# Packed score rows and DMA-carried splits in the second attention of a two-layer encoder

## The chip, the cores and the metric

One core of a Trainium2 chip runs the kernel. The metric is the device time of one execution in microseconds. TensorE multiplies matrices: it holds up to 128x128 weights and streams up to 512 columns past them, into banks of PSUM. VectorE (DVE), ScalarE (ACT) and GpSimd (POOL) work element by element; SyncE (SP) issues transfers. In the profile, PE is TensorE's matmuls and PEld its weight loads.

## The reference

Two layers on x of 1024 positions by 1024 features. Each computes `u = x*(1+scale)+shift` and `x = LayerNorm(alpha*x + gate*mixer(u))`. Layer 0 mixes by a dilated windowed attention of 18 heads. Layer 1, where the change lies, mixes by a latent attention of 16 heads:

```
cq, ckv, k_rope, gate = split(u @ w_in, [256, 384, 416])
q  = rmsnorm(cq) @ w_uq        # per head: 64 plain values, 32 rotary ones
kv = rmsnorm(ckv) @ w_ukv      # per head: 64 key values, 64 value columns
q_rope, k_rope = rope(q_rope), rope(k_rope)     # k_rope is shared by all heads
s  = (q_nope . k_nope + q_rope . k_rope) * 96**-0.5
y  = softmax(s) @ v * silu(gate) @ w_out
```

So a score is a dot product over 96 values: 64 of the head and 32 rotary ones.

## The kernel before, in words

Nearly every product is made from split numbers: a float32 value is held as a rounded high part h (type fp32r) and the rest l, and `mm3` (lines 90 to 94) makes a product as three matmuls, h·h, h·l and l·h. A split is a copy by ACT, which rounds, and a subtraction by DVE or POOL.

The program runs layer A's projections and attention, layer A's gate and output, then layer B. `layer_b_in` (from line 1015) makes the latents of eight blocks of 128 positions (`latents`, and `latents_t`, which transposes them), and then eight gate blocks of two halves each (`gate`, line 1116), 24 matmuls a half; `weave` (line 49) alternates two generators in proportion to their weights. The 16 heads go in eight pairs p:

- `b_turn(p)` (line 1238), once for two pairs (four heads), multiplies out the rotary part of the queries for both halves of the positions, turns it with the cosine and sine table cs, and leaves the rows in tiles `ab` and `rope`.
- `b_qk(p)` (line 1265) makes queries and keys of the pair for each half of 512 positions. A product of 128 rows holds both heads, 64 rows each; each head's rows are split by a 64-row copy and a 64-row subtraction of their own (lines 1278, 1279, 1304, 1306). The rotary rows are split by ACT (1285) and POOL (1287) into rows 64 to 127. `b_rope_rows` (1224) copies the rotary key rows of a head's tiles to the tiles of the next but one by a POOL transfer.
- `b_v` makes the values of four heads.

A head has a high and a low query tile and a high and a low key tile, each of 128 rows: 64 plain ones and 64 for the 32 rotary values and zeros. `latents_t` writes the first key rows.

`layer_b_attention` (1316) goes over 128 units u; a unit is a head and 128 of its queries. `front(u)` makes the scores of the unit against 1024 keys: `mm3` for each half of the keys, so six matmuls over 128 rows (line 1328). `soft` takes the row maximum (DVE, 1336), `expo` the exponential (ACT, 1344), `middle(u-2)` transposes the weights two units later, eight transposes, splits them into pth (ACT, 1379) and ptl (DVE, 1380), and `back` multiplies two units' weights with the values, 16 matmuls (1396), whose output ACT copies (1405, 1406). In each turn of the loop comes first `front(u)`, then `middle(u-2)`, then `expo(u)`, and in every second turn `back`. Steps of `b_turn` and `b_qk` of the next pair (the generator prep) and of `b_v` (vprep) are put between them: `b_turn` starts at unit 2 of every second pair, `b_qk` at unit 8 of a pair's 16.

PSUM holds two score tiles s of two banks each and four banks t, which transposes, outputs and up-projections share. SBUF tiles of 4 KB a row come from two pools, G with 33 and H with 14.

The order on TensorE and SP is that of the code (`FIXED`, line 42). The order on ACT, DVE and POOL is chosen when the program is built, by the readiness of the operations there with the order of the code as priority; on the chip each engine goes through its list in order. The denominators of the softmax go through DRAM: SP writes `den_d` and reads it spread over 64 rows (`spread`, lines 1358 and 1359), and POOL multiplies (1365).

Of the kernel before, what the change touches and what calls it, by code (L numbers as in the profile page):

```python
# [69 lines left out]
class Trunk:  # L70
# [944 lines left out]
    def layer_b_in(self):  # L1015
# [11 lines left out]
        self.kb = [[self.ht(F32R, "kb") for _ in range(2)] for _ in range(2)]  # L1027

# [22 lines left out]
        nc.gpsimd.memset(latn, 0.0)  # L1051
        ln = [latn[:, 0:512], latn[:, 512:1024]]

        def latents(i):
# [8 lines left out]
            tmp = self.M.tile([P, 64], F32, tag="krt", bufs=2, name=self.nm("krt"))  # L1063
# [19 lines left out]
        def latents_t(i):  # L1083
            t, c = ln[i % 2], i * P
            pt = self.bank("plt")
            for j in range(4):
                nc.tensor.transpose(pt[:, j * P : j * P + P], t[:, j * P : j * P + P], self.ident)
            dst = [(h[:, c : c + P], l[:, c : c + P], slice(0, P), j) for j, (h, l) in enumerate(self.lat)]
            for e, (h, l) in enumerate(self.kb):
                dst.append((h[64:128, c : c + P], l[64:128, c : c + P], slice(64 - 64 * e, 128 - 64 * e), 3))  # L1090
            for h, l, rows, j in dst:
                src = pt[rows, j * P : j * P + P]
                nc.scalar.copy(h, src)
                nc.vector.tensor_tensor(l, src, f32(h), op=ALU.subtract)

# [18 lines left out]
        self.wu, self.wv, self.q, self.gT = {}, {}, {}, []  # L1114
# [16 lines left out]
        for b in range(8):  # L1131
            if b + 2 < 8:
                gq[b + 2] = self.bw_load(b + 2)
            for _ in gate(b, 0, self.bank if b < 2 else self.mbank):
                pass
# [10 lines left out]
            if b == 0:  # L1146
                self.kb.append([self.ht(F32R, "kb") for _ in range(2)])
                self.b_rope_rows(2)
            if b == 1:
                gate1 = self.ada_last()  # L1150
            if b == 2:
# [3 lines left out]
                self.cs = self.ht(F32, "cs")  # L1155
                nc.sync.dma_start(self.cs, A["qtab"])
# [67 lines left out]
    def b_rope_rows(self, hd):  # L1224

        for src, dst in zip(self.kb[(hd - 2) % 3], self.kb[hd % 3]):
            self.nc.gpsimd.dma_start(dst[64:128, :], src[64:128, :])
# [9 lines left out]

    def b_turn(self, p):


        nc = self.nc
        r1 = self.ht(F32, "rope")
        self.rope = {p: [], p + 1: [r1[64:128, 0:512], r1[64:128, 512:1024]]}
        for hf in range(2):
# [10 lines left out]
            r0 = ab[64:128, 512:1024]  # L1255
            for dst, row, op in (
                (r1[64:96, sl], 32, ALU.subtract),
                (r1[96:128, sl], 96, ALU.add),
                (r0[32:64], 64, ALU.add),
                (r0[0:32], 0, ALU.subtract),  # L1260
            ):
                nc.gpsimd.tensor_tensor(dst, ab[row : row + 32, 0:512], ab[row : row + 32, 512:1024], op=op)
            self.rope[p].append(r0)

    def b_qk(self, p):

# [4 lines left out]
        qe = [self.gt(F32R, "q") for _ in range(2)]  # L1271
        qo = [self.gt(F32R, "q") for _ in range(2)]
        self.q[2 * p], self.q[2 * p + 1] = qe, qo
        ke, ko = self.kb[(2 * p) % 3], self.kb[(2 * p + 1) % 3]
        rr = self.rope.pop(p)

        def put(dst, sl, src):
            nc.scalar.copy(dst[0][0:64, sl], src)
            nc.vector.tensor_tensor(dst[1][0:64, sl], src, f32(dst[0][0:64, sl]), op=ALU.subtract)

        def rope(hf, part):
            sl = slice(hf * 512, hf * 512 + 512)
            for q in (qe, qo):
                if part == 0:
                    nc.scalar.activation(q[0][64:128, sl], rr[hf], AF.Copy)
                else:
                    nc.gpsimd.tensor_tensor(q[1][64:128, sl], rr[hf], f32(q[0][64:128, sl]), op=ALU.subtract)

        if p:
            self.b_rope_rows(2 * p)  # L1290
            self.b_rope_rows(2 * p + 1)
        for hf in range(2):
# [3 lines left out]
            put(qe, sl, ps[0:64, :])  # L1296
            put(qo, sl, ps[64:128, :])
            yield 0.0
            rope(hf, 0)
# [3 lines left out]
            for n, k in enumerate((ke, ko)):  # L1303
                nc.scalar.copy(k[0][0:64, sl], ps[64 * n : 64 * n + 64, :])
            for n, k in enumerate((ke, ko)):
                nc.vector.tensor_tensor(
                    k[1][0:64, sl], ps[64 * n : 64 * n + 64, :], f32(k[0][0:64, sl]), op=ALU.subtract
                )
            rope(hf, 1)
# [6 lines left out]
    def layer_b_attention(self):  # L1316
# [4 lines left out]
        def front(u):  # L1321
            hd, t = u // 8, u % 8
            q, k = self.q[hd], self.kb[hd % 3]
            s = self.PB.tile([P, 1024], F32, tag="s", bufs=2, name=self.nm("s"))
            ts = slice(t * P, t * P + P)
            for j in range(2):
                ks = slice(j * 512, j * 512 + 512)
                self.mm3(s[:, ks], q[0][:, ts], q[1][:, ts], k[0][:, ks], k[1][:, ks], True, True)
            if t == 7:
                self.q.pop(hd)  # L1330
            st[u] = s
# [81 lines left out]
        for u in range(nu + 4):  # L1413
            p, r = u // 16, u % 16
            if u < nu:
                front(u)
                next(prep, None)
                next(vprep, None)
                soft(u)
            if p + 1 < NPAIR_B:  # L1420
                if r == 1:
                    self.b_weights(p + 1)
                if p % 2 and r == 2:
                    prep = self.b_turn(p + 1)
                if r == 8:
                    prep = self.b_qk(p + 1)
            elif u < nu:
                if r in (1, 3, 5, 7):
                    self.b_wo_load((r - 1) // 2)
                elif r in (4, 6, 8, 10):  # L1430
                    self.b_wo_split((r - 4) // 2, nc.gpsimd)
                if r in (10, 11, 12, 13):
                    self.b_yt(r - 10, 0)
                elif r in (14, 15):
                    for b in (2 * r - 24, 2 * r - 23):
                        self.b_wo_load(b)
            if 0 <= u - 2 < nu:
                middle(u - 2)
                next(vprep, None)
            if u < nu:  # L1440
                expo(u)
            if u == nu:
                self.b_rows()
                self.b_out_blocks(0, range(4))
            if u == nu + 1:
                self.b_out_blocks(1, range(4))
            if u >= 4 and u % 2 == 0 and u < nu + 4:
                back((u - 4) // 2)
            if u >= 11 and u % 4 == 3:
                normalise((u - 11) // 4)  # L1450
            if u % 32 == 2 and 32 < u < nu:
# [228 lines left out]
```

## Time and profile before

| | before |
|---|---|
| median of 3 runs | 1356.2 us (1355.8 to 1360.3) |
| the profiled execution | 1356.85 us, span 1355.1 |
| TensorE clock granted | 0.994 of full speed |
| second attention, first to last score | 776.0 to 1244.0 us |
| scores (tile s, lines 92 to 94) | 768 matmuls |
| their row maximum | 128 times, 1217 ns |
| their exponential | 128 times, 1126 ns |
| DMA queues, all stages | 114.30 MB, mean 84 GB/s |

A row of the groups names line, engine, operation, output and inputs, shapes and count, then busy time and the mean duration of one in ns, then the idle time of the engine just before them and what ended it. A row of busy time by stage has the stretch, its length, and for each engine busy time and instructions. A row of the instructions in order of time has start and duration in us. A row of the waits has who waited for whom, the sum, how often, and the longest.

### The profile page before, as it was taken

What the parts mean: (1) busy time and instruction counts of PE and PEld (TensorE: products, weight loads), DVE (VectorE), ACT (ScalarE), POOL (GpSimd) and SP (SyncE); (2) the same over time, 40 slices, a digit from 0 to 9 for tenths busy, and PEclk for the clock granted to TensorE, in tenths of its full rate; (3) what the DMA queues carried; (4) which work ended last, traced back from release to release, by engine and by line L of the source; (5) the groups of instructions that cost most, each with busy time, mean ns of one, the idle gap of its engine ahead of it and who ended that gap; (6) DMA issues with size and microseconds to landing.
All of it is one profiled execution on the core that took longest, in us unless ns stands there. A gap on an engine that the chain in (4) does not pass through costs nothing.

```text
span 1355.1 us, 20458 instructions
## 1 busy us (share of the span) xinstructions
PE 1328.6 (98%) x7435; PEld 1143.5 (84%) x7435; DVE 855.9 (63%) x1480; ACT 799.1 (59%) x1631; POOL 565.3 (42%) x552
## 2 busy tenths in 40 slices
PE   9999999999999999999999999999999999999997
PEld 7888888888888888888988888898889889898776
DVE  7645445445544345376733378878787788777887
ACT  4665556544444423165632397889698878887411
POOL 0333123213231477425533444734654473444861
PEclk8999999999999999999999999999999999999999
DMA  9423211113244374371163011111121111113322
GB/s 369 146 35 64 33 58 54 49 27 126 96 132 132 92 179 160 124 252 47 50 182 115 2 33 34 24 38 25 32 52 28 30 25 28 25 55 124 110 93 93
DMA packets 45117, 114.30 MB, mean 84 GB/s; under 512 B 6893, under 2 KB 13342, under 8 KB 45017
## 3 DMA queue, kind: packets, MB, share of 16 engines
q1 hardware_dynamic: 40204, 100.41, 24.0%
q0 software_dynamic: 4192, 12.27, 3.7%
q8 instruction: 59, 0.97, 0.3%
q14 instruction: 42, 0.34, 0.1%
q10 hardware_dynamic: 620, 0.31, 0.1%
HBM read 96.43 MB, written 8.67 MB: 78 GB/s over the span
## 4 chain that ended last, share of the span: by engine, by line
PE 78%; DVE 7%; ACT 7%; DMA 3%; issue 3%; SPq 0%; ACTq 0%; DVEq 0%
PE pj L92 8%; PE pj L94 8%; PE pj L93 8%; PE o L1396 6%; PE t L1376 5%; PE po L92 4%; PE po L93 4%; PE po L94 4%; PE s L92 3%; PE s L94 3%; PE s L93 3%; PE pg L92 2%; PE pg L93 2%; PE pg L94 2%; PE ip L272 2%
## 5 line engine op out<-in xcount | busy, mean ns | idle before, releaser
L92 PE MATMUL pj<-uh,wh 128*128 128x512 f32 x528 | 217.2, 411 | 0.7 <-ACT wh L104 0.7
L94 PE MATMUL pj<-uh,wl 128*128 128x512 f32 x528 | 207.0, 392 | 0.0
L93 PE MATMUL pj<-ul,wh 128*128 128x512 f32 x528 | 206.8, 392 | 0.0
L1336 DVE TENSOR_REDUCE mb<-s 128x1 f32<-128x1024 f32 x128 | 155.8, 1217 | 48.7 <-PE s L94 47.9
L1380 DVE TENSOR_TENSOR ptl<-t,pth 128x512 fp32r<-128x512 f32 x256 | 165.3, 681 | 5.2 <-ACT pth L1379 3.0
L1379 ACT CAST pth<-t 128x512 fp32r<-128x512 f32 x256 | 139.5, 590 | 37.4 <-PE t L1376 34.0
L1344 ACT ACTIVATE pr<-s,mb 128x1024 f32<-128x1024 f32 x128 | 144.2, 1126 | 15.4 <-DVE mb L1336 14.7
L105 POOL TENSOR_TENSOR wl<-wraw,wh 128x1024 fp32r<-128x1024 f32 x42 | 106.3, 2536 | 102.4 <-ACT wh L104 75.4
L1376 PEld LDWEIGHTS t<-ident,pr 128*128 128x128 f32 x1024 | 119.3, 141 | 19.1 <-DVE ptl L1380 2.8
L1376 PE MATMUL t<-ident,pr 128*128 128x128 f32 x1024 | 133.1, 273 | 2.1 <-DVE ptl L1380 2.1
L1396 PE MATMUL o<-pth,vq 128*128 128x256 f32 x512 | 130.4, 292 | 1.1 <-DVE ptl L1380 1.1
L1396 PE MATMUL o<-ptl,vq 128*128 128x256 f32 x512 | 125.6, 283 | 0.8 <-DVE ptl L1380 0.5
L564 ACT ACTIVATE sb<-sb,stat 128x256 f32<-128x256 f32 (+1 forms) x144 | 67.0, 466 | 94.8 <-DVE stat L558 94.7
L94 PEld LDWEIGHTS pj<-uh,wl 128*128 128x128 f32 x528 | 99.1, 188 | 22.2
L1407 POOL TENSOR_TENSOR osum<-osum 64x256 f32<-64x256 f32 x64 | 47.9, 748 | 163.7 <-ACT osum L1406 162.6
L92 PEld LDWEIGHTS pj<-uh,wh 128*128 128x128 f32 x528 | 99.7, 189 | 15.1 <-ACT wh L104 1.1
L93 PEld LDWEIGHTS pj<-ul,wh 128*128 128x128 f32 x528 | 99.8, 189 | 14.0
L92 PE MATMUL s<-kb,q 128*128 128x512 f32 x256 | 105.8, 413 | 0.1
L94 PE MATMUL s<-kb,q 128*128 128x512 f32 x256 | 100.4, 392 | 0.0
L93 PE MATMUL s<-kb,q 128*128 128x512 f32 x256 | 100.4, 392 | 0.0
L1396 PEld LDWEIGHTS o<-ptl,vq 128*128 128x128 f32 x512 | 97.8, 191 | 1.7 <-DVE ptl L1380 1.7
L1396 PEld LDWEIGHTS o<-pth,vq 128*128 128x128 f32 x512 | 97.6, 191 | 1.8 <-DVE ptl L1380 1.7
(289 smaller groups left out, 3128.2 us busy)
## 6 DMA issues: line engine op xcount, KB each, us to landing
wraw<-wa SPq DMA_DIRECT2D x36, 512.0 KB
ada<-ada_row SPq DMA_DIRECT2D x64, 256.0 KB
wraw<-wo_a SPq DMA_DIRECT2D x18, 512.0 KB
ada<-ada_ss SPq DMA_DIRECT2D x16, 512.0 KB
kb<-kb POOLq DMA_DIRECT2D x30, 256.0 KB, 4.5
f<-f_d SPq DMA_DIRECT2D x18, 256.0 KB
xr<-x SPq DMA_DIRECT2D x8, 512.0 KB
xn_d<-z POOLq DMA_DIRECT2D x8, 512.0 KB, 4.5
```

Source lines behind the costliest of these rows:

```text
L92: mm(out, wh, xh, start=start, stop=False)
L93: mm(out, wh, xl, start=False, stop=False)
L94: mm(out, wl, xh, start=False, stop=stop)
L105: (lo_engine or self.nc.gpsimd).tensor_tensor(l[:, :width], raw[:, :width], f32(h[:, :width]), op=ALU.subtract)
L564: nc.scalar.activation(sb[:, a * w : a * w + w], sb[:, a * w : a * w + w], AF.Exp, bias=stat[:, 0, hh, t : t + 1], scale=-1.0, accum_out=s ...
L1336: nc.vector.tensor_reduce(m[:, 0:1], s, axis=AX.X, op=ALU.max, negate=True)
L1344: nc.scalar.activation(pr, s, AF.Exp, bias=m[:, 0:1], accum_out=dens[u // 8][:, u % 8 : u % 8 + 1])
L1376: nc.tensor.transpose(pt[:, c * P : c * P + P], pr[:, kt * P : kt * P + P], self.ident)
L1379: nc.scalar.copy(h, src)
L1380: nc.vector.tensor_tensor(l, src, f32(h), op=ALU.subtract)
L1396: nc.tensor.matmul(po[:, 0:256], v, pts[j][x][:, c * 256 : c * 256 + 256], start=n == 0, stop=n == 15)
L1407: nc.gpsimd.tensor_tensor(w3[mine, 0:256], w3[mine, 256:512], w3[mine, 0:256], op=ALU.add)
```

## The change

The scores of a unit take three passes over 96 values each, 288 rows of products. The change packs them into two full passes and a quarter:

- The query tile qa holds a head's high rows and below them its low rows; the key tile k[0] holds the high key rows twice. One matmul gives h·h + l·h of the plain part.
- qb holds the high plain rows and below them 32 high and 32 low rotary rows; k[1] holds the low plain key rows and 32 low and 32 high rotary key rows. One matmul gives h·l of the plain part and both mixed terms of the rotary part.
- What is left, h·h of the rotary part, takes 32 rows. Four such matmuls (two units, two halves of the keys) are issued one behind another at the row positions 0, 32, 64 and 96 of the array, from a tile q3 (four copies of the rotary query rows, for alternating units) and a tile kr (four copies of the rotary key rows).

So `front` works on two units at a time: four full matmuls, the four small ones, four full ones. The loop goes in steps of two units: front of both, both maxima, `expo` of the first, `middle(u0-2)`, `expo` of the second, `back`, `middle(u0-1)`.

For all pairs but the first, `b_qk` splits queries and keys as 128 rows at once, into a staging tile hl (one ACT copy, one DVE subtraction), and SP transfers carry the 64-row pieces to their places. `b_turn` adds up the rotary rows as 64 rows at once, splits them as 128, and SP writes them to a DRAM tile, from which qb and q3 are read. The first rotary rows (`b_turn(0)`) are made beside the first half of gate 7 rather than beside the second halves of gates 6 and 7; for them DVE does what POOL does for the later ones. The rotary key rows of k[1] are written once for the three key buffers. The table cs is read anew for each `b_turn`.

The diff, cut to its core:

```diff
@@ layer_b_in
+        self.kr = self.M.tile([P, 512], F32R, name="kr")
...
-            for c in (400, 448):
-                nc.vector.tensor_tensor(t[:, c : c + 16], tmp[:, 0:16], tmp[:, 32:48], op=ALU.subtract)
-                nc.vector.tensor_tensor(t[:, c + 32 : c + 48], tmp[:, 16:32], tmp[:, 48:64], op=ALU.add)
+            rot = t[:, 384:512].rearrange("p (g a c) -> p g a c", g=4, a=2)
+            x = [tmp[:, 16 * n : 16 * n + 16].unsqueeze(1).to_broadcast([P, 4, 16]) for n in range(4)]
+            nc.vector.tensor_tensor(rot[:, :, 0, :], x[0], x[2], op=ALU.subtract)
+            nc.vector.tensor_tensor(rot[:, :, 1, :], x[1], x[3], op=ALU.add)
...
+            first = gate(b, 0, self.bank if b < 2 else self.mbank)
...
+                weave((first, 5184.0), (self.b_turn(0), 2600.0))
...
-        weave((chain(gate(6, 1, self.mbank), gate(7, 1, self.mbank)), 10368.0), (chain(self.b_turn(0), self.b_qk(0)), 9000.0))
+        weave((chain(gate(6, 1, self.mbank), gate(7, 1, self.mbank)), 10368.0), (self.b_qk(0), 4500.0))
@@ b_rope_rows
+        dma, first = self.nc.gpsimd.dma_start, self.kb[0][1]
+        for j in range(2):
+            dma(first[96:128, j * 512 : j * 512 + 512], self.kr[32 * j : 32 * j + 32, :])
+        for n in (1, 2):
+            dma(self.kb[n][1][64:128, :], first[64:128, :])
@@ b_turn
-                nc.gpsimd.tensor_tensor(dst, ab[row : row + 32, 0:512], ab[row : row + 32, 512:1024], op=op)
-            self.rope[p].append(r0)
+            engine = nc.gpsimd if p else nc.vector
+            for rows, op in ((slice(0, 64), ALU.subtract), (slice(64, 128), ALU.add)):
+                engine.tensor_tensor(ab[rows, 0:512], ab[rows, 0:512], ab[rows, 512:1024], op=op)
+            yield 0.0
+            hl = self.ht(F32R, "rope")
+            nc.scalar.activation(hl[:, 0:512], ab[:, 0:512], AF.Copy)
+            engine.tensor_tensor(hl[:, 512:1024], ab[:, 0:512], f32(hl[:, 0:512]), op=ALU.subtract)
+            for a in range(2):
+                for x in range(2):
+                    nc.sync.dma_start(rd[:, x, a, :, sl], f32(hl[64 * a : 64 * a + 64, x * 512 : x * 512 + 512]))
@@ b_qk
+            nc.sync.dma_start(f32(qb[64:128, :]), rows.rearrange("x a c t -> (x a c) t"))
+            q3 = third[:, e * 512 : e * 512 + 512]
+            for g in range(4):
+                src = rows[0].rearrange("a c (i z t) -> (a c) i z t", z=2, t=P)[:, :, g // 2, :]
+                nc.sync.dma_start(f32(q3[32 * g : 32 * g + 32, :]).rearrange("p (i t) -> p i t", t=P), src)
...
+            if p:
+                hl = self.ht(F32R, "hl")
+                nc.scalar.copy(hl[:, 0:512], ps)
+                nc.vector.tensor_tensor(hl[:, 512:1024], ps, f32(hl[:, 0:512]), op=ALU.subtract)
+                for x in range(2):
+                    for e in range(2):
+                        src = f32(hl[64 * e : 64 * e + 64, x * 512 : x * 512 + 512])
+                        for t, rows in places[e][x]:
+                            nc.sync.dma_start(f32(t[rows, sl]), src)
+                return
...
+        q_at = [(((qa, up), (qb, up)), ((qa, down),)) for qa, qb, k in heads]
+        k_at = [(((k[0], up), (k[0], down)), ((k[1], up),)) for qa, qb, k in heads]
@@ layer_b_attention, front
-                self.mm3(s[:, ks], q[0][:, ts], q[1][:, ts], k[0][:, ks], k[1][:, ks], True, True)
+            def full(a):
+                ts = slice((t + a) * P, (t + a) * P + P)
+                for n, (q, kk) in enumerate(((qa, k[0]), (qb, k[1]))):
+                    for j in range(2):
+                        ks = slice(j * 512, j * 512 + 512)
+                        mm(s[a][:, ks], q[:, ts], kk[:, ks], start=n == a == 0, stop=n == a == 1)
+                st[u + a] = s[a]
+
+            full(0)
+            for g in range(4):
+                rows = slice(32 * g, 32 * g + 32)
+                ks = slice((g % 2) * 512, (g % 2) * 512 + 512)
+                mm(
+                    s[g // 2][:, ks], q3[rows, (t // 2) * P : (t // 2) * P + P], self.kr[rows, :],
+                    start=g >= 2, stop=g < 2, tile_position=(32 * g, 0),
+                )
+            full(1)
@@ layer_b_attention, the loop
+        for u0 in range(0, nu + 4, 2):
+            if u0 < nu:
+                front(u0)
                 next(prep, None)
                 next(vprep, None)
...
+                soft(u0)
+                soft(u0 + 1)
+                expo(u0)
+            for u in (u0, u0 + 1):
...
+                if 0 <= u - 2 < nu:
+                    middle(u - 2)
+                    next(vprep, None)
+                if u == u0 and u < nu:
+                    expo(u + 1)
+                if u == u0 and u >= 4:
+                    if u % 32 == 4:
+                        for _ in vprep:
+                            pass
+                    back((u - 4) // 2)
...
+                next(vprep, None)
+                next(prep, None)
+            next(prep, None)
             next(vprep, None)
```

More of the change, by code (lines that the diff above doesn't have):

```diff
@@ L1270, in b_qk @@
         ch, cl = self.lat[2]
[L1271 to L1287, printed above, removed]
@@ new lines, in split @@
+        def split(ps, sl, places):
+            if p:
[3 more added lines that the diff above has]
+                for x in range(2):
+                    for e in range(2):
+                        src = f32(hl[64 * e : 64 * e + 64, x * 512 : x * 512 + 512])
+                        for t, rows in places[e][x]:
+                            nc.sync.dma_start(f32(t[rows, sl]), src)
+                return
+            for e in range(2):
+                src = ps[64 * e : 64 * e + 64, :]
+                for t, rows in places[e][0]:
+                    nc.scalar.copy(t[rows, sl], src)
+            for e in range(2):
+                (t, rows), = places[e][1]
+                h, hr = places[e][0][0]
+                nc.vector.tensor_tensor(t[rows, sl], ps[64 * e : 64 * e + 64, :], f32(h[hr, sl]), op=ALU.subtract)
@@ L1295, in b_qk @@
             yield 1300.0
-            put(qe, sl, ps[0:64, :])
-            put(qo, sl, ps[64:128, :])
+            split(ps, sl, q_at)
             yield 0.0
-            rope(hf, 0)
             ps = self.mbank()
@@ L1302, in b_qk @@
             yield 650.0
[L1303 to L1309, printed above, removed]
+            split(ps, sl, k_at)
             yield 0.0
```

130 lines of the change are left out of this document (60 added, 70 removed).

## The prediction

> **What bounds the kernel now.** I read the page first, then busy time by stage, then the waits of TensorE in the second attention, then its instructions in order of time.
>
> ```profile
> span 1355.1 us, 20458 instructions
> PE 1328.6 (98%) x7435; PEld 1143.5 (84%) x7435; DVE 855.9 (63%) x1480; ACT 799.1 (59%) x1631; POOL 565.3 (42%) x552
> ```
> ```profile
> 640.00:700.00 60.00, 60.00 (x328) 55.92 (x328) 34.31 (x147) 36.02 (x112) 33.74 (x33) 1.00 0.31 92
> 700.00:760.00 60.00, 59.31 (x262) 48.81 (x261) 16.89 (x18) 12.46 (x19) 12.44 (x6) 1.00 0.33 104
> 776.00:1249.00 473.00, 466.15 (x3077) 415.31 (x3076) 378.01 (x516) 399.37 (x787) 235.12 (x250) 1.00 0.15 36
> ```
> ```profile
> PE m L92 <- DVE kb L1306: 3.3, 7, 0.5
> PE t L1376 <- DVE ptl L1380: 2.1, 3, 0.8
> PE o L1396 <- DVE ptl L1380: 1.1, 2, 0.8
> ```
>
> The change lies in the second attention, the row from 776 to 1249 us: 473.0 us, in which TensorE is busy for 466.15 and waits for data for 3.3 + 2.1 + 1.1 us (those are all the entries of PE there). So this stage lasts as long as TensorE takes to issue its matmuls. But ACT (399.37 us) is busy for 84% of the stage and DVE (378.01) for 80%: they hide behind TensorE with little to spare. A busy TensorE says nothing of its pace, since matmuls overlap; the pace is read from the starts:
>
> ```profile
> 1011.71 0.48 PE L92 MATMUL s<-kb,q 128*128 128x512 f32 x1
> 1012.03 0.39 PE L93 MATMUL s<-kb,q 128*128 128x512 f32 x1
> 1012.26 0.40 PE L94 MATMUL s<-kb,q 128*128 128x512 f32 x1
> ...
> 1013.18 1.04 PE L1376 MATMUL t<-ident,pr 128*128 128x128 f32 x8
> 1013.97 0.36 PE L1396 MATMUL o<-pth,vq 128*128 128x256 f32 x1
> ...
> 1017.36 1.04 PE L1376 MATMUL t<-ident,pr 128*128 128x128 f32 x8
> 1018.15 0.47 PE L92 MATMUL s<-kb,q 128*128 128x512 f32 x1
> ```
>
> This is one round of two units (a unit is 128 queries of one head): six score matmuls, eight transposes, sixteen value products, six scores, eight transposes; 1018.15 - 1011.71 = 6.44 us. Scores start 0.23 us apart, though each is shown as 0.39 long, so 0.16 us of each overlaps the next. The first score after transposes takes 0.32, that is 0.09 more. Eight transposes, each with a load of 128 weight columns of its own, show as 1.04 us, of which the last takes 0.27, so they go (1.04 - 0.27)/7 = 0.11 us apart. There are 64 rounds, 412 us; the other 61 us are the up-projections (tile m).
>
> **Scores: what TensorE saves.** Twelve matmuls a round stay twelve. Eight are full ones at 0.23: 1.84 us. The other four take 32 rows each, at four places of the array and into four banks, and everything hangs on T, the time from the first of them to the next full one. No row of before shows a matmul on part of the rows, so T is bounded. Lowest: the four streams run side by side, one spacing, 0.23. Highest: one after another with the array emptied before and after: 4 x 0.23 + 2 x 0.16 = 1.24. The nearest row is the transposes': four loads of 128 columns at 0.11 are 0.44, and I add the 0.09 that the trace shows where the kind of matmul changes: T = 0.53. Then a round takes 6.44 - 12 x 0.23 + 1.84 + 0.53 = 6.05 us for TensorE, 0.39 less, and 64 x 0.39 = 25 us in all. With the lowest T it would be 6.44 - 0.92 + 0.23 = 5.75.
>
> **Scores in pairs: what ACT and DVE give back.** Both units' scores now come first, and the two score buffers fill together. These rows give ACT's and DVE's own pace:
>
> ```profile
> 1033.97 1.07 ACT L1379 CAST pth<-t 128x512 fp32r<-128x512 f32 x2 [1.08 <-PE t L1376]
> 1034.93 1.13 ACT L1344 ACTIVATE pr<-s,mb 128x1024 f32<-128x1024 f32 x1
> ...
> 1038.95 0.37 ACT L1405 COPY osum<-o 64x256 f32<-64x256 f32 x1
> 1039.34 0.37 ACT L1406 COPY osum<-o 64x256 f32<-64x256 f32 x1
> ...
> 1041.67 1.12 ACT L1344 ACTIVATE pr<-s,mb 128x1024 f32<-128x1024 f32 x1
> ...
> 1042.78 1.06 ACT L1379 CAST pth<-t 128x512 fp32r<-128x512 f32 x2
> ```
> ```profile
> 1033.54 1.23 DVE L1336 TENSOR_REDUCE mb<-s 128x1 f32<-128x1024 f32 x1 [1.05 <-PE s L94]
> 1034.68 1.28 DVE L1380 TENSOR_TENSOR ptl<-t,pth 128x512 fp32r<-128x512 f32 x2
> 1035.87 1.22 DVE L1336 TENSOR_REDUCE mb<-s 128x1 f32<-128x1024 f32 x1
> ```
>
> Start to start, a cast takes 0.48 us (0.96 for two), an output copy 0.39, an exponential 1.11 (1041.67 to 1042.78), a maximum 1.14 and a subtraction 0.60 (1.19 for two). A round needs of ACT 2 x 1.11 + 4 x 0.48 + 2 x 0.39 = 4.92 us and of DVE 2 x 1.14 + 4 x 0.60 = 4.68: each fits into 6.05. But they also wait for each other in turn. If both keep the order of the new code, the ring is: maximum of the first unit (1.23 and 0.02 to be seen), then all of ACT's round (exponential, two casts, exponential, two copies, two casts: 4.92), the last cast's end (1.07 - 0.96 = 0.11), the last subtraction (0.60), and only then the next round's maximum: 1.25 + 4.92 + 0.11 + 0.60 = 6.88 us. That is more than the 6.44 of today, where each unit has its own maximum and its two casts lie ahead of its exponential. The order on ACT and DVE is not in the diff: it is chosen at build, by what is ready. If one cast slips ahead of the first exponential, which has to wait for its maximum, the ring is 6.88 - 0.48 = 6.40. If the next maximum also slips ahead of the last subtraction, it falls by the last cast too, to 5.92, below TensorE's 6.05. Of these I expect the last two in turn, since the idle time that the last rows show ahead of an operation (1.08 and 1.05 us) is where such slips go: half-way between 6.05 and 6.40, 6.22 us a round, 0.22 less than now. 64 x 0.22 = 14 us. So 11 of TensorE's 25 us are given back.
>
> **Rows of queries and keys.** Groups of the attention, for the splits that are replaced:
>
> ```profile
> L1379 ACT CAST pth<-t 128x512 fp32r<-128x512 f32 x254 | 138.4, 590 | 37.4 <-PE t L1376 34.0
> L1278 ACT CAST q<-m 64x512 fp32r<-64x512 f32 x28 | 16.3, 582 | 5.4 <-DVE q L1279 5.2
> L1285 ACT ACTIVATE q<-rope 64x512 fp32r<-64x512 f32 x16 | 9.2, 620 | 0.2
> L1306 DVE TENSOR_TENSOR kb<-m,kb 64x512 fp32r<-64x512 f32 x29 | 19.9, 687 | 1.6 <-ACT kb L1304 1.4
> L1287 POOL TENSOR_TENSOR q<-rope,q 64x512 fp32r<-64x512 f32 x16 | 20.3, 1293 | 4.3 <-ACT q L1285 4.0
> L1227 POOL DMA_DIRECT2D kb<-kb x26 | 14.3, 558 | 0.0
> ```
>
> A 128-row cast (590 ns) costs what a 64-row one does (582). For each half of a pair after the first, ACT goes from four casts of 0.58 and two rotary ones of 0.62, 3.6 us, to two of 0.59, 1.2; DVE from four subtractions of 0.69 to two. Over 14 halves that is 34 us less on ACT and 19 on DVE; POOL loses two subtractions of 1.29 a half, 36 us, and its 26 key-row issues, 14 us. None of it is on TensorE's path: it is worth nothing directly, and is what lets me leave the rounds that carry up-projections at no further stall. TensorE makes the same up-projection matmuls.
>
> **Transfers.** In exchange SP gets 24 transfers from staging and 10 rotary ones a pair, and 8 more for every second pair.
>
> ```profile
> kb<-kb POOLq DMA_DIRECT2D x26, 256.0 KB, 4.5
> ```
> ```profile
> SPq L1358 <- ACT rden L1357: 406.8, 31, 19.3
> ```
> ```profile
> 1011.27 0.45 SPq L1359 DMA_DIRECT2D rden<-den_d  x1
> ```
>
> At 0.45 us an issue, 34 are 15 us of a pair's 16 units (8 x 6.2 = 50 us), and SP now does little but wait for the denominators (406.8 us). What is queued behind a transfer that waits for its subtraction is the next pair's rows and the denominators' write and read, which only POOL needs. The last key rows are split after the scores of unit 12 of a pair and are needed at unit 16, two rounds or 12.4 us later: cast and subtraction some 2.5, six issues 2.7, landing 4.5, together 9.7. So I cost it at nothing, with 2.7 us in hand; the bounds are nothing and one landing at each of seven pair starts, 7 x 4.5 = 32 us.
>
> **Start.** The first rotary rows move into a stage in which DVE has idled (16.89 of 60 us busy), so their eight products and the sums, now on DVE, cost nothing there:
>
> ```profile
> 760.86 0.68 DVE L1252 TENSOR_TENSOR ab<-m,cs 64x512 f32<-64x512 f32 x1 [25.90 <-PE m L94]
> ```
>
> The first pair's splits go straight from the bank, eight casts a half: two more for each of queries and keys than now, and the last two may hold up the first score by 2 x 0.58. I take 1 us, between 0 and 2. The key rows beside the latents change by a few small operations under a TensorE that is busy for 60.00 of 60.00 us: nothing.
>
> **Sum.** The profiled execution took 1356.85 us (span 1355.1 and 1.75 around it), 0.65 above the median of the runs. 1356.85 - 14 + 1 = 1343.9, predicted as 1344.
>
> **Rivals.** *The ring in the order of the code (slower).* TensorE waits each round in the value products for the last subtraction and in the scores for the exponential. 64 x (6.88 - 6.44) = 28 us; in rounds with up-projections TensorE itself is longer, which may hide half. I take 21: 1356.9 + 21 + 1 = 1379. It decides once a maximum sits behind both last subtractions. For it: ACT and DVE in the quoted rows keep to the order of the code. Against: there the order of readiness is the same, so they don't tell. Chance 0.18.
>
> *The small matmuls cost as much as they replace (no change).* If the array empties before and after the four, T = 0.53 + 2 x 0.16 = 0.85, the round 6.37 and the ring 6.40: 64 x 0.04 = 3 us gained, 1355; one after another without loads hidden it would be up to 1.24, 0.32 more than now, 64 x 0.32 = 20 us lost. For it: the 0.09 us at each change of kind in the rows. Against: 0.09 is far from 0.32. Chance 0.13, 0.10 of it within 0.3%, 0.03 slower. The Trainium skill, TensorEngine Tiling (Array Packing), "Key Properties", speaks for this one: a change of tiling mode drains TensorE, and here there are two a round.
>
> *All of it (faster still).* T = 0.23 and the ring at 5.92, which then bounds: 64 x (6.44 - 5.92) = 33 us, 1325. Chance 0.11. The Trainium skill, TensorE: Matmul & The Clock Gate, "Measured speedup vs the span model", is near it: four row tiles of 32 with 512 columns went 3.07 times as fast, so by it T would be an estimated 0.92/3.07 = 0.30. No row here shows which of the two holds.
>
> *Rows that land late.* The 32 us above against a gain of 13: 1376. Chance 0.05 (0.03 slower, 0.02 within).
>
> **How the numbers follow.** The forecast has 0.53, its own range from TensorE's 6.05 alone (25 us, 1333) to the ring of 6.40 (3 us, 1355): 0.50 of it faster, 0.03 within. Two runs differ by up to 0.3%, 4 us, so I count that as no change. Faster: 0.50 + 0.11 = 0.61; within: 0.03 + 0.10 + 0.02 = 0.15; slower: 0.18 + 0.03 + 0.03 = 0.24. The range goes from 1325 to 1380: outside lie half of the gain in full and nearly half of the ring.
>
> **What would show it.** Right: the starts around the four small matmuls some 0.5 us apart in total; rounds of about 6.2 us; a new wait of TensorE, in all 10 to 15 us, for ptl from DVE or for pr from ACT; PE's share of the stage falls while ACT and DVE go above 85%. Wrong in T: rounds of 6.4 without waits, or waits alone below 5.8. Wrong in the ring: a wait of TensorE of over 40 us with a maximum behind two subtractions. Wrong in the transfers: a wait of the first score of a pair for a DMA into q or kb.

## The result: 1.2% slower, and the profile after

The changed kernel takes 1373.46 us (median of 4 runs, 1371.63 to 1374.57), the kernel before 1356.8 us (4 runs, 1355.8 to 1360.3): a ratio of 1.0117, with a 95% interval of 1.0094 to 1.0139. The forecast was 1344. The profiled execution took 1372.57 us. Two executions among the experiments stand far outside, one of 5119 and one of 1612 us: the medians below include them, the ratios do not.

The top of the page, the stage row for the same window as before, and TensorE's longest waits in the second attention (line, releaser, total us, times, longest):

```profile
span 1370.7 us, 20847 instructions
...
PE 1327.2 (97%) x7435; PEld 1110.2 (81%) x7435; DVE 845.9 (62%) x1434; ACT 770.2 (56%) x1583; POOL 491.2 (36%) x479
```
```profile
776.00:1249.00 473.00, 451.01 (x2982) 371.39 (x2980) 348.65 (x470) 355.89 (x713) 167.35 (x181) 0.98 0.36 92
```
```profile
PE s L1364 <- DMA kb<-hl: 8.9, 5, 3.0
PE o L1442 <- DVE ptl L1426: 3.2, 6, 1.1
PE t L1422 <- ACT osum L1452: 2.7, 7, 0.6
PE t L1422 <- DVE ptl L1426: 2.5, 4, 0.8
PE s L1364 <- DMA q<-rope_d: 2.2, 1, 2.2
```

ACT, DVE and POOL all have less to do, as forecast, and TensorE's busy time hardly moves (1328.6 to 1327.2). Two rows are new: the scores wait for rows of keys (kb) and of queries (q) that a DMA carries, 11.1 us together. That is the sign that the prediction named for "wrong in the transfers". The clock granted to TensorE is 0.98 in this window where it was 1.00.

To see where the time lies, take the start of the first score matmul of every round from TensorE's timeline (line 92 before, line 1364 after) and subtract. A pair of heads is 8 rounds. Sums by pair, in us (the last pair has 7 differences):

| | pair 0 | 1 | 2 | 3 | 4 | 5 | 6 | 7 | all |
|---|---|---|---|---|---|---|---|---|---|
| before | 54.1 | 60.8 | 59.7 | 60.8 | 59.7 | 61.2 | 59.7 | 47.0 | 463.0 |
| after | 60.5 | 59.8 | 64.6 | 59.6 | 64.2 | 59.7 | 62.9 | 46.8 | 478.0 |
| first round, before | 5.61 | 6.44 | 6.44 | 6.43 | 6.44 | 6.43 | 6.43 | 6.44 | |
| first round, after | 9.95 | 6.33 | 12.71 | 6.33 | 12.33 | 6.32 | 11.00 | 6.32 | |

The stage is 15.0 us longer. The first rounds of pairs 0, 2, 4 and 6 alone are 4.3 + 6.3 + 5.9 + 4.6 = 21 us longer; everything else together is 6 us shorter. So the rest of the stage does gain, and four places take more than that back.

**A plain round** of the changed kernel, from TensorE's timeline:

```profile
1073.35 1.09 PE L1364 MATMUL s<-kb,q 128*128 128x512 f32 x4
...
1079.40 1.17 PE L1364 MATMUL s<-kb,q 128*128 128x512 f32 x4
1080.49 0.50 PE L1371 MATMUL s<-kr,q 32*128 32x512 f32 x4
1080.92 1.19 PE L1364 MATMUL s<-kb,q 128*128 128x512 f32 x4
1081.95 1.03 PE L1422 MATMUL t<-ident,pr 128*128 128x128 f32 x8
...
1085.77 0.47 PE L1364 MATMUL s<-kb,q 128*128 128x512 f32 x1
```

The rounds here last 6.05 and 6.37 us (1073.35 to 1079.40 to 1085.77). All scores of the second take 1081.95 - 1079.40 = 2.55 us; before, two sets of six took 2 x 1.47 = 2.94, from the prediction's rows. That is 0.39 us less, the forecast's figure. The four small ones take 0.43, and the full ones before and after them some 0.1 more each than their own pace gives (1.09 after transposes and 1.03, where four matmuls at 0.23 are 0.92 and the change from transposes is 0.09). In the trace the four small ones start within 0.01 us of one another.

**A bad round**, the first of pair 2, and the clock around it (after TensorE's busy time come the loads, DVE, ACT, POOL, then the granted clock, the DMA share and GB/s):

```profile
897.39 0.47 PE L1364 MATMUL s<-kb,q 128*128 128x512 f32 x1
899.93 0.71 PE L1364 MATMUL s<-kb,q 128*128 128x512 f32 x2 [2.06 <-DMA kb<-hl]
901.74 0.79 PE L1364 MATMUL s<-kb,q 128*128 128x512 f32 x1 [1.10 <-DMA kb<-hl]
...
903.19 2.08 PE L1364 MATMUL s<-kb,q 128*128 128x512 f32 x4
...
905.07 1.91 PE L1422 MATMUL t<-ident,pr 128*128 128x128 f32 x8
...
910.10 1.17 PE L1364 MATMUL s<-kb,q 128*128 128x512 f32 x4
```
```profile
900.00:901.00 1.00, 0.64 (x2) 0.21 (x2) 0.00 (x0) 0.00 (x0) 0.07 (x1) 1.00 1.00 223
901.00:902.00 1.00, 0.26 (x1) 0.26 (x1) 0.00 (x0) 0.00 (x0) 0.00 (x0) 0.68 0.78 174
...
907.00:908.00 1.00, 1.00 (x6) 1.00 (x6) 0.78 (x2) 0.94 (x2) 0.00 (x0) 0.50 0.00 0
908.00:909.00 1.00, 1.00 (x10) 1.00 (x9) 0.37 (x1) 0.76 (x2) 0.00 (x0) 0.90 0.00 0
```

TensorE stands still for 2.06 + 1.10 = 3.2 us. Then the granted clock is 0.50 until about 908.1, and four full matmuls show 2.08 us instead of 1.19: from 901.7 on, 6.4 us at half speed lose another 3.2. The two make 6.4, against the 6.3 by which the round is longer. The wait rows show only the first half of it. The same holds for pairs 0, 4 and 6, whose granted clock is 0.50 from 781.9 to 785.3, from 1024.3 to 1031.0 and from 1150.6 to 1153.9 us: over the four places the waits are 11.1 us and the half clock takes nearly as much again. The Trainium skill, TensorE: Matmul & The Clock Gate, "Why this matters for your kernels", warns of idle gaps of about 3 us, after which the clock falls to half; pair 2 agrees, with 3.2 us of waits and 0.50, but at the start of pair 0 one wait of 2.2 us was enough.

**Who was late**, on SP's timeline (start, us, line):

```profile
851.00 0.27 SPq L1404 DMA_DIRECT2D den_d<-rden  x1
852.23 0.47 SPq L1405 DMA_DIRECT2D rden<-den_d  x1
858.67 10.67 SPq L1281 DMA_DIRECT2D rope_d<-rope  x8
869.44 0.55 SPq L1404 DMA_DIRECT2D den_d<-rden  x1
875.31 0.51 SPq L1405 DMA_DIRECT2D rden<-den_d  x1
876.12 0.49 SPq L1298 DMA_DIRECT2D q<-rope_d  x1
...
882.50 3.74 SPq L1316 DMA_DIRECT2D q<-hl  x6
886.34 3.77 SPq L1316 DMA_DIRECT2D kb<-hl  x6
...
892.52 4.25 SPq L1316 DMA_DIRECT2D q<-hl  x6
896.81 3.16 SPq L1316 DMA_DIRECT2D kb<-hl  x5
```
```profile
SPq L1405 <- DMA den_d<-rden: 42.8, 30, 5.5
```

The last split of the pair's keys, from DVE's timeline:

```profile
885.00 0.69 DVE L1311 TENSOR_TENSOR hl<-m,hl 128x512 fp32r<-128x512 f32 x1
```

Between the write of the denominators (line 1404) and their read (line 1405) lie 1.2 us at 851, but 5.9 at 869, behind the eight rotary writes (line 1281). SP waits there, and the rows of pair 2 queue behind it: they begin at 876.12, with the reads of the rotary rows, which need those same writes. From then on SP issues almost without a pause: ten rotary reads, twelve rows, the denominators again (890.20 to 892.52), twelve rows. An issue of a staged row costs 3.74/6 = 0.62 us where the forecast had 0.45. So the last keys, which are split by 885.69, stand in the queue for 11 us: their six issues run from 896.81 to 900.6, while the scores want them at 897.4. (SP's last row above shows five of them, since the stretch ends at 900 us.) Pairs 1, 3, 5 and 7 have no rotary writes of their own, and their first rounds are undisturbed.

### The profile page after: what moved, and what is told of

Its sections match the earlier page's. It is cut to its first block, busy times and chain, and to the rows that moved or that the text cites. A ratio compares the mean times of both kernels' runs of the same rounds, so it can differ in the third digit from the quotient of the medians.

```text
span 1370.7 us, 20847 instructions
## 1 busy us (share of the span) xinstructions
PE 1327.2 (97%) x7435; PEld 1110.2 (81%) x7435; DVE 845.9 (62%) x1434; ACT 770.2 (56%) x1583; POOL 491.2 (36%) x479
## 4 chain that ended last, share of the span: by engine, by line
PE 75%; DVE 10%; ACT 7%; issue 4%; DMA 3%; SPq 1%; DVEq 0%; ACTq 0%; POOL 0%
PE pj L92 8%; PE pj L94 8%; PE pj L93 8%; PE o L1442 5%; PE s L1364 5%; PE t L1422 4%; PE po L92 4%; PE po L94 4%; PE po L93 4%; DVE mb L1382 3%; ACT pr L1390 2%; PE ip L272 2%; PE pg L92 2%; PE pg L94 2%; PE pg L93 2%
## 5 line engine op out<-in xcount | busy, mean ns | idle before, releaser
L1426 DVE TENSOR_TENSOR ptl<-t,pth 128x512 fp32r<-128x512 f32 x256 | 168.5, 683 | 59.1 <-ACT pth L1425 58.5
L1390 ACT ACTIVATE pr<-s,mb 128x1024 f32<-128x1024 f32 x128 | 143.1, 1119 | 72.2 <-DVE mb L1382 62.9
L1364 PE MATMUL s<-kb,q 128*128 128x512 f32 x512 | 155.6, 424 | 11.6 <-DMA kb<-hl 8.9
L1422 PE MATMUL t<-ident,pr 128*128 128x128 f32 x1024 | 139.0, 277 | 5.8 <-ACT osum L1452 2.9
L1364 PEld LDWEIGHTS s<-kb,q 128*128 128x128 f32 x512 | 89.4, 192 | 42.7 <-issue 21.7
L104 ACT ACTIVATE wh<-wraw 128x1024 fp32r<-128x1024 f32 x54 | 57.1, 1058 | 46.1 <-DMA wraw<-wa 25.0
```

The lines of the kernel that those rows point to most:

```text
L1364: mm(s[a][:, ks], q[:, ts], kk[:, ks], start=n == a == 0, stop=n == a == 1)
L1390: nc.scalar.activation(pr, s, AF.Exp, bias=m[:, 0:1], accum_out=dens[u // 8][:, u % 8 : u % 8 + 1])
L1422: nc.tensor.transpose(pt[:, c * P : c * P + P], pr[:, kt * P : kt * P + P], self.ident)
```

## The experiments

Three theories: A, SP is held behind the rotary writes, which land slowly by their shape; B, SP simply has too many issues; C, ACT's and DVE's order (the forecast's ring) is what costs. Where nothing else is said, a kernel is the changed one with the edit shown. "Before" is 1358.46 us for the first four kernels and 1357.24 for the others.

### Rotary rows with 16 as the slowest size

```diff
-nc.sync.dma_start(rd[:, x, a, :, sl], f32(hl[64 * a : 64 * a + 64, x * 512 : x * 512 + 512]))
+nc.sync.dma_start(rd[:, x, a, :, sl].rearrange("h c t -> c h t"), f32(hl[64 * a : ...]))
-wr = uq[..., 64:96].reshape(2, P, 4, 2, 2, 2, 16).transpose(2, 1, 0, 5, 3, 4, 6).reshape(4, P, 256)
+wr = uq[..., 64:96].reshape(2, P, 4, 2, 2, 2, 16).transpose(2, 1, 0, 5, 6, 3, 4).reshape(4, P, 256)
-a["qtab"] = c(np.concatenate([cos] * 4 + [sin] * 4, 1).T)
+a["qtab"] = c(np.concatenate([np.repeat(cos, 4, 1), np.repeat(sin, 4, 1)], 1).T)
```

The weights' columns and the tables are put in another order, so that a staging tile's rows run over the 16 components first and the 4 heads second. Every engine issues the same instructions in the same order as in the changed kernel; only the shape of these writes differs.

> Rotary rows laid out so that each write to DRAM has 16 as its slowest size instead of 4; nothing else changes. Theory A, the rotary writes are slow and hold SP: the eight writes land in 3 us instead of 7, the wait of the denominators' read behind them falls from 6 to about 1.2 us, the first rounds of pairs 0, 2, 4 and 6 lose most of their 21 us, total 1355 to 1360. Theory B, SP has too many transfers to issue whatever their shape (34 a pair at 0.62 us): first rounds change by under 2 us each, total 1366 to 1372. Theory C, the order on ACT and DVE makes each round long: no change, 1372.

> The rotary rows with 16 as the slowest size once more, beside the kernel with both edits on the same chip: 1352 to 1357 by theory A, as before; a difference of under 2 us to the kernel with both edits.

Measured: 1354.32 us (10 runs, 1351.77 to 1359.04), ratio to before 0.9967 (0.9949 to 0.9986), and in a second set 1353.89 (11 runs), 0.9976 (0.9965 to 0.9986). That is some 19 us below the changed kernel. The busy share of the DMA engines (next to last column) while the rotary writes before pair 2 land, first the changed kernel (both halves of the positions), then the edited one (the second half); the rows and rounds of the edited kernel are those of the second set's profile:

```profile
864.00:865.00 1.00, 1.00 (x10) 1.00 (x10) 1.00 (x2) 0.45 (x2) 1.00 (x2) 1.00 0.29 100
...
873.00:874.00 1.00, 1.00 (x8) 0.82 (x7) 0.11 (x1) 0.98 (x5) 0.00 (x0) 1.00 0.22 83
874.00:875.00 1.00, 1.00 (x10) 0.91 (x9) 0.42 (x1) 1.00 (x3) 0.00 (x0) 1.00 0.12 38
```
```profile
864.00:865.00 1.00, 1.00 (x7) 0.49 (x6) 0.32 (x2) 0.96 (x4) 0.00 (x0) 1.00 0.43 148
865.00:866.00 1.00, 1.00 (x7) 0.79 (x6) 1.00 (x2) 0.93 (x2) 0.88 (x2) 1.00 0.64 213
866.00:867.00 1.00, 1.00 (x10) 0.84 (x8) 1.00 (x3) 0.87 (x1) 0.57 (x1) 1.00 0.10 35
```
```profile
855.12 9.80 SPq L1281 DMA_DIRECT2D rope_d<-rope  x8
865.02 0.43 SPq L1404 DMA_DIRECT2D den_d<-rden  x1
866.64 0.48 SPq L1405 DMA_DIRECT2D rden<-den_d  x1
```
```profile
SPq L1405 <- DMA den_d<-rden: 33.4, 32, 1.6
```

The changed kernel's writes keep the share near a quarter until 874.5 us, 5 us after SP has issued the last of them (858.67 + 10.67 = 869.3). With 16 as the slowest size the share reaches 0.64 and the writes are through soon after 866, before SP reads the denominators at 866.64; the longest wait there falls from 5.5 to 1.6 us. A quarter is four of 16 engines, and four is the number of heads, the slowest size of the write. The Trainium skill, DMA: Bandwidth & Descriptors, "Rules for kernel authors", states this rule: the count of engines follows from the slowest size that isn't one, and a size below 16 in front confines the transfer. Both shapes here agree. The denominators' own write has 4 rows too; that it queues on the very engines of the rotary writes would explain its 5.5 us, but no run shows which engines served it.

The first rounds of pairs 0, 2, 4 and 6 are now 6.37, 7.31, 6.68 and 6.73 us, and the stage from first to last round 456.8, where it was 463.0 before and 478.0 after the change (458.2 in the first set's profile, which is that set's slowest execution). The rows of pair 2 begin 25.3 us ahead of the pair's first score instead of 21.3. Theory A holds. B alone can't explain the gain, since the issues are as many, nor can C, since every engine's order is the same.

### Queries and keys split straight from the bank

```diff
-            if p:
+            if False:
```

No staging tile and no DMA: for every pair, ACT and DVE write 64 rows at a time, as the changed kernel does for the first pair only.

> All pairs split queries and keys straight from the bank, as the first pair does; the 24 staging transfers a pair are gone, ACT makes 8 casts a half instead of 2 and DVE 4 subtractions instead of 2. Theory A: waits for staging rows vanish, but the start and the held denominators stay and ACT gets about 48 us more: 1368 to 1380. Theory B: the first rounds of pairs 2, 4, 6 return to 6.3 us, 17 us less, of which ACT takes some back: 1358 to 1366. Theory C: ACT's extra casts lengthen every round with projections: 1385 or more.

Measured: 1394.73 us (1394.29 to 1395.0), 1.0264 (1.0248 to 1.0279). By its time this is theory C's forecast (1385 or more); A's and B's ranges are both missed. The first rounds of pairs 2, 4 and 6 are 6.66, 6.65 and 6.66, so with 24 issues fewer a pair even the slow rotary writes come in time. But the rounds with up-projections grow; the sixth and seventh of pair 2 go from 8.53 and 6.06 to 10.13 and 8.30 us. ACT's busy time between 1000 and 1200 us (fourth of the busy columns), here and with the rotary rows at 16:

```profile
1000.00:1200.00 200.00, 186.85 (x1239) 152.07 (x1238) 152.09 (x204) 163.94 (x326) 64.29 (x73) 0.99 0.13 39
```
```profile
1000.00:1200.00 200.00, 196.79 (x1353) 164.42 (x1350) 154.28 (x207) 155.22 (x312) 68.75 (x78) 1.00 0.38 97
```

ACT does more while TensorE gets through 1239 matmuls instead of 1353. So the carried rows are worth 21 us even with the slow writes, and 40 us against the kernel with fast ones: scores in pairs leave little room for the narrow splits. Some 5 us of it are clock: after waits of TensorE of 2.4 to 2.6 us in the third rounds of pairs 1, 3 and 5, the granted clock is 0.50 for 3.4 us each time.

### Rows started two units earlier

```diff
-                    if r == 8:
+                    if r == 6:
                         prep = self.b_qk(p + 1)
```

> The next pair's projections begin at unit 6 of a pair instead of 8, one round (6.3 us) earlier, nothing else. Theories A and B both: the rows of pairs 2, 4 and 6 are 6 us earlier and their first rounds lose about 5 us each, the start stays: 1357 to 1361. Theory A alone would say less where SP is still held at unit 6 by the denominators' read: 1361 to 1368. Theory C: 1372.

Measured: 1370.7 us (median of 4), 1.0087 (1.0067 to 1.0107). A miss for A and B. The number is near C's 1372, but not because nothing changes. The first rounds of pairs 2, 4 and 6 fall to 6.17, and with them these pairs from 64.6, 64.2 and 62.9 us to 59.5, 59.6 and 59.7. But pairs 1, 3 and 5, which had lost nothing, grow from 59.8, 59.6 and 59.7 to 62.3, 62.2 and 62.0, in the rounds to which the up-projections move (fourth and fifth of pair 3: 9.63 and 9.70 us, from 6.98 and 8.49). Pair 0 stays at 9.83 in its first round. SP's wait for the denominators stays too:

```profile
SPq L1405 <- DMA den_d<-rden: 44.5, 31, 5.2
```

An earlier start hides the wait without removing it, and costs elsewhere. Why pairs 1, 3 and 5 grow was not settled: the order on ACT and DVE is another in this build, and TensorE has a new wait, 6.2 us in all, for the staging subtraction.

### Denominators on POOL's queue

```diff
-            nc.sync.dma_start(den_d[v].rearrange("(a b) -> a b", b=P), rows)
-            nc.sync.dma_start(t[mine, :], den_d[v : v + 1, :].to_broadcast([64, 512]))
+            nc.gpsimd.dma_start(den_d[v].rearrange("(a b) -> a b", b=P), rows)
+            nc.gpsimd.dma_start(t[mine, :], den_d[v : v + 1, :].to_broadcast([64, 512]))
```

> The denominators are written and read back by POOL's queue instead of SP's. Theory A: SP is no longer held by the read behind the rotary writes, so the next pair's rows start 6 us earlier before pairs 2, 4, 6: 1357 to 1362, the start unchanged. Theory B: one of 34 issues less, 1369 to 1373. Theory C: no change; POOL waiting for the landing may cost up to 5 us.

Measured: 1359.89 us (10 runs), 1.0013 (1.0003 to 1.0022). The first rounds of pairs 2, 4 and 6 are 6.47, 6.34 and 6.34: with the rotary writes as slow as ever, nothing is lost there once the denominators are out of SP's queue. Pair 0 keeps its 10.25, for its rotary rows still come too late:

```profile
PE s L1364 <- DMA q<-rope_d: 2.4, 1, 2.4
```

Yet SP is still held. Its next entry, the read of the rotary rows, now waits for the writes itself, four times where it was once (7.2 us) in the changed kernel:

```profile
SPq L1298 <- DMA rope_d<-rope: 25.4, 4, 7.4
```

The rows of pair 2 begin 24.1 us ahead of the pair's first score instead of 21.3, and nothing stands between their two halves, where the denominators took 2.3 us. So the last key row is issued 0.9 us before the first score, and not 3.2 after it. The denominators' wait is thus not the whole of theory A: the rotary rows need the slow writes in any case, and what the edit removes is a few us of a queue that is full. The order on ACT and DVE is also another in this build, so the edit is not alone in it.

### Both edits

> The rotary rows laid out with 16 as the slowest size, and also the denominators' write and read issued by POOL. Theory A (the loss was SP held behind the slow rotary writes): nothing is left for the second edit, 1352 to 1356, the first rounds of pairs 2, 4 and 6 at 6.4 to 7.0 us. Theory B (SP also has too many issues, whatever their shape): a further 3 to 6 us go when SP has 64 issues fewer, 1348 to 1351.

Measured: 1354.33 us (11 runs), 0.998 (0.9971 to 0.9988), beside 1353.89 for the rotary rows at 16 alone on the same chip. In total the 64 issues less on SP bring nothing, and B's 1348 to 1351 is missed. But the first rounds of pairs 2, 4 and 6 do fall once more, to 6.32, 6.33 and 6.34 us (1.7 us together), while pairs 1, 3 and 5 grow from 58.6 to 61.6, 60.5 and 60.5. ACT and DVE have another order in this build than with the rotary rows at 16 alone, and TensorE's wait for the output copies is 10.7 us instead of 4.4. So B is no rival for the 19 us, but that the number of issues costs nothing is not shown: with the fast writes too the last key row of pair 2 is issued 0.5 us after the pair's first score.

### The small matmuls left out, and issued twice

Both start from the rotary rows at 16. What the small matmuls hold is h·h of the rotary part: left out, the scores lack it; twice, it counts double. In both the start and stop flags are set to match.

```diff
-            for g in range(4):
+            for g in range(0):
```
```diff
-            for g in range(4):
+            for i in range(8):
+                g = i % 4
```

> With the rotary rows at 16 as base (1354), the four small score matmuls are left out, so the rotary low parts of the scores are missing. Theory P (TensorE sets the round of 6.2 us): each round loses the four loads and two changes of shape, 0.65 us, 64 x 0.65 = 42 us, about 1313. Theory R (the ring of ACT and DVE sets the round, as the forecast had it): the round stays at 6.1 to 6.2, the time at 1346 to 1354, and TensorE's waits for ptl and pr grow by what it saves.

> With the rotary rows at 16 as base (1354), the four small score matmuls are issued twice in a row, so the rotary low parts count double. Theory P: a round grows by one more set at 0.43 us without a further change of shape, 64 x 0.43 = 28 us, about 1382. Theory R: the ring's slack hides part of it, under 15 us more, below 1369. If a set of four costs one after another (4 x 0.23 = 0.92): 59 us more, about 1413.

Measured: left out 1337.4 us (1335.67 to 1341.2), 16.5 below its base; twice 1392.55 (1392.13 to 1393.88), 38.7 above it. TensorE's timeline with them left out, then with them twice:

```profile
997.25 2.10 PE L1364 MATMUL s<-kb,q 128*128 128x512 f32 x8
999.18 1.04 PE L1422 MATMUL t<-ident,pr 128*128 128x128 f32 x8
```
```profile
1103.65 1.17 PE L1364 MATMUL s<-kb,q 128*128 128x512 f32 x4
1104.74 0.74 PE L1372 MATMUL s<-kr,q 32*128 32x512 f32 x8
1105.41 1.19 PE L1364 MATMUL s<-kb,q 128*128 128x512 f32 x4
```

Without them the scores take 1.93 us instead of 2.55, so T as the sum uses it is 0.62 a round, 40 us in 64 rounds. Only 16.5 show: the rounds of the pairs go to 5.4 and 6.6 in turn, and TensorE's wait for the last subtraction grows:

```profile
PE o L1442 <- DVE ptl L1426: 13.4, 21, 1.2
```

It was 3.4 us in the base. So neither theory holds alone: TensorE paces the round of about 6.2, but ACT and DVE stand close behind, and of TensorE time saved beyond this less than half comes out. This goes for the order that this build chose for ACT and DVE, which is not the base's.

Twice, the set takes 0.67 (1104.74 to 1105.41) instead of 0.43: a second set of four adds 0.24, one spacing of a full matmul. The four stream side by side; the rest of T, 0.62 - 0.24 = 0.38, goes with getting into and out of that shape. 64 x 0.24 is 15 us. Of the other 23, TensorE's waits make 15 (27.9 us in all, from 12.6), and two stretches of 3.4 us at a granted clock of 0.50, from 866.5 and from 1122.5 us, cost 3.4 together; the rest is not assigned. TensorE's waits for the output copies, and ACT's for the maximum, were 4.4 and 47.9 us in the base:

```profile
ACT pr L1391 <- DVE mb L1383: 78.0, 42, 2.4
...
PE t L1423 <- ACT osum L1453: 17.8, 15, 2.8
```

Between 1100 and 1108 us ACT's order is there: exponential, cast, exponential, cast, two copies, two casts, then 2.0 us of waiting for the next maximum, 7.13 us from exponential to exponential (1100.78 to 1107.91). That is close to the prediction's ring in code order, 6.88. DVE's order closes the ring: there both maxima come ahead of all four subtractions, while in most of the base's plain rounds the second maximum comes between them. The order is chosen at build, and the eight matmuls were enough to change it. So this kernel's time is not the price of the matmuls alone.

## Why the prediction was wrong, point by point

**Transfers: the step that failed.** The prediction weighed SP's issues and the landing of the last key rows, found 9.7 of 12.4 us needed, "So I cost it at nothing", with bounds from 0 to 32 us. It cost 21 in the first rounds of pairs 0, 2, 4 and 6. The step that failed is the path of the last key rows: it was added up from their own split, issues and landing, as if the queue were empty when they came. They were split in time, 11.7 us ahead of the pair's first score, and then stood in SP's queue for 11 us. Three things filled it. The issue is 0.62 us and not 0.45; the forecast took the price of a different transfer. The rotary writes keep about a quarter of the DMA engines busy, four heads being the slowest size, and so are in flight for another 5 us after SP has issued them; the pair's first rows, read from what they write, and the denominators' read ahead of these both wait for them. And the denominators' write and read stand between the rows as well as behind them. The run with the rotary rows at 16, in which nothing but the shape of these writes differs, shows that without this delay the queue is done nearly in time. About half of the price, 3.2 of 6.4 us in pair 2, is the half clock after the stall, for which the sum had no term. The rival *Rows that land late* came near the time, 1376 against 1373.5 measured, and got a chance of 0.05. Its size was in part luck: it priced one landing of 4.5 us at each of seven pair starts, and the runs show waits and half clock at four places, one of them pair 0.

**Scores.** The 0.39 us that TensorE saves in a round came out as 0.39. That is luck: T was forecast at 0.53 and is 0.62; in exchange one of two changes of shape after transposes goes, which the sum had left out, and the two errors of 0.09 cancel. What the prediction quotes from the Trainium skill is seen in part. That changing the mode drains TensorE (TensorEngine Tiling (Array Packing), "Key Properties") fits the 0.38 us that a set costs beyond its streaming, 0.19 for each of two changes if they are alike. That four row tiles run together (TensorE: Matmul & The Clock Gate, "Measured speedup vs the span model") is seen in the 0.24 for a second set; but with its two changes a set takes 0.62, and not the 0.30 that the prediction estimated from that page.

**The ring.** Forecast: 6.22 us a round. The plain rounds range from 6.05 to 6.37, and with the small matmuls left out two rounds average 6.0, a pace of ACT and DVE in that build's order. Right in size, but the signs that the prediction named came only in part: with the rotary rows at 16, TensorE's waits for ptl and pr sum to 6 us and not 10 to 15, and ACT and DVE are busy for 78 and 77% of the stretch from 1000 to 1200 us, less than before, and not above 85%. The round of 6.05 shown above has no wait at all. The ring in code order exists, but in the kernel with doubled matmuls, not in this one.

**The sum over the attention.** 14 us were forecast as gain. With the rotary writes mended the stage is 463.0 - 456.8 = 6.2 us shorter. The other 8 are in rounds that the sum took to gain like all others. Pair 0 takes 56.9 instead of 54.1 us, of which 0.8 is a wait for a split made straight from the bank and 1.2 are waits around the start of its third round for exponentials, which the scores of two units at a time need done; the second rounds of pairs 2, 4 and 6, in which value products of the next four heads are made, take 10.6 instead of 9.6; the first rounds of these pairs are still 0.2 to 0.9 over what they were. These make 2.8 + 3.0 + 1.4 = 7.2. For pair 0 and the value products, the prediction's "no further stall" for rounds with up-projections was too kind. What holds up the value products' rounds was not tried by itself.

**Rows of queries and keys.** That the relief of ACT and DVE lets the pairs of scores run is borne out by the 21 to 40 us that the direct splits cost. That POOL's relief is worth nothing was not tried.

**Start.** The first score starts at 777.1 instead of 776.2 us: 0.9 against a forecast of 1. This is no confirmation: the two profiles of the kernel with the rotary rows at 16 start at 777.2 and 781.8 us. The first round is 4.3 us longer, 2.2 us of it a wait for the rows of pair 0; 3.6 of the 4.3 go with the rotary rows at 16.

## What to carry to other kernels

When work moves to a DMA queue, walk that queue in order, with the time of every issue, and ask of each entry what it waits for and what is queued behind it: rows that were split in time stood in this queue for 11 us. Check the slowest size of every transfer's access pattern, since with a size of 4 the DMA engines were a quarter busy here and one reordering of constant weights and tables mended it. Look at the granted clock after a stall of TensorE: stalls of 2 to 3 us cost about twice here what the wait rows show.

## What the runs showed of the hardware

- After 3.2 us of waits between 897.9 and 901.7 us, TensorE's granted clock fell to 0.50 and stayed there for some 6.4 us of steady work. After one wait of 2.2 us, from 777.7 to 779.9, it was 0.50 from 781.9 to 785.3.
- Four matmuls of 32 rows at four row positions, 512 columns, stream in the time of one full matmul (0.24 us for a second set), but a single set between full matmuls costs 0.62 us, so 0.38 goes with the two changes of shape.
- SP needs 0.62 us to issue a 64-row transfer from one on-chip tile to another (3.74 us for six), where the denominators' read costs it 0.47.
- Writes of 128 KB with 4 as the slowest size hold the mean busy share of the 16 DMA engines at 0.22 to 0.29; with 16 it reaches 0.64.
